# Weight splits and adaLN steps held in source order on VectorE, in a hybrid trunk block

## The chip, the cores and the metric

The kernel runs on one core of a Trainium2 chip. The time is device microseconds of one execution. Lower is better. One execution was also recorded by the hardware profiler; the rows shown below come from that record.

## The reference

One layer of a decoder trunk for 256 tokens of width 2048, all in f32. A conditioning vector c gives six modulation vectors (adaLN); the token mixer runs a retention branch and a short convolution branch side by side, and a gated feed-forward part with a causal convolution follows.

```python
mod = silu(c) @ w_ada + b_ada                      # 2048 x 12288
sh1, sc1, g1, sh2, sc2, g2 = split(mod, 6)
xn = rmsnorm(h, norm1_g) * (1 + sc1) + sh1
q, k, v, g_ret, bg, cg, xc, gates = split(xn @ w_in)
y_ret  = (retention(rotary(q), rotary(k), v) * silu(g_ret)) @ w_ret_o
y_conv = (bg * causal_conv3(cg * xc, w_sc)) @ w_conv_o
ga, gb = split(sigmoid(gates + b_gate))
h = h + g1 * ((ga * y_ret + gb * y_conv) @ w_mix_o)
xn2 = rmsnorm(h, norm2_g) * (1 + sc2) + sh2
gt = causal_conv3(xn2 @ w_gate, w_ffconv, b_ffconv)   # 5632 wide
h = h + g2 * ((silu(gt) * (xn2 @ w_up)) @ w_down)
out = rmsnorm(h, final_g)
```

## The kernel before

**Split products.** Every matrix product is made of rounded f32 pieces. A weight tile of 256 rows by 512 columns arrives in a buffer `raw` (SyncE's DMA queue, lines 291 and 323; six buffers). ScalarE rounds it into `hi` (L300), VectorE takes the rest, `lo = raw - hi` (L301). TensorE multiplies with both. Activations are split in the same way by `split` (L92 on ScalarE, L93 on VectorE).

**Units.** The program is a list of units, walked by one loop. A `Weights` unit is one such tile with its products. In `w_block` a unit issues, for each of four outputs, two matmuls with `hi` (L405, 512 columns) and two with `lo` (L410, 256 columns). Eight units make a block of 512 output columns; after the last unit ScalarE copies half of each output out of PSUM (L416) and an `epilogue` runs for each of the four. An `Ada` unit multiplies a weight tile of w_ada by the conditioning vector and adds it to an accumulator `ada` on VectorE (L335 for the first row tile, L337 for the others); it has no products on TensorE. Ada units are spread between the others until the second norm. A `Call` unit runs a helper.

**Stages.** Ten blocks in the first stage (values, swish gate, first query and key block), then the other query and key blocks with retention, the merge gates with the retention output, the convolution branch, the merge gates with the convolution output (`conv_o_block`, L797 to L800, then a split L92 and L93), the mixer output, the second norm, and the feed-forward part: eleven pairs of a gate block and an up block (`ff_blocks`, epilogues `e_g` L912 to L921 and `e_u` L924 to L926) and two rounds of down blocks.

**What sets the order.** The loop loads nine units ahead and calls `prep` (the casts and differences) two units ahead of `run`, in the first stage four ahead. So in the source the `lo` of unit n+2 is written after the products and the epilogue of unit n-1 and before those of unit n. The framework then reorders the instructions of each engine by when it reckons their operands to be ready. Each engine takes its instructions in the order that results. `tc.keep_in_program_order(x)` holds x behind the instruction that was written just before it for the same engine; it adds no wait for data.

The pools `hi` and `lo` have three buffers each, so `hi` and `lo` can be at most three units ahead of the products.

Of the kernel before, what the change touches and what calls it, by code (L numbers as in the profile page):

```python
# [10 lines left out]
F32 = mybir.dt.float32  # L11
# [4 lines left out]
ALU = mybir.AluOpType  # L16
# [30 lines left out]
def tile_trunk_block(  # L47
# [6 lines left out]
    nc = tc.nc  # L54
# [16 lines left out]
    def nm(s):  # L71
        serial[0] += 1
        return f"{s}_{serial[0]}"
# [7 lines left out]
    def blk8(name, shape, dtype):  # L81
        return big.tile(shape, dtype, tag="b8", name=nm(name))
# [43 lines left out]
    c_act = const.tile([P, KT], F32, name="c_act")  # L126
# [140 lines left out]
    class Call:  # L267
# [6 lines left out]
        def prep(self):  # L274
            if self.fn["prep"]:
                self.fn["prep"]()
# [5 lines left out]
    class Weights:  # L282
# [10 lines left out]
        def prep(self):  # L293
            if self.in_big:
                both = blk8("hl", [P, 2, UK, CB], F32R)
                self.hi, self.lo = both[:, 0], both[:, 1]
            else:
                self.hi = wpool.tile([P, UK, CB], F32R, tag="hi", bufs=3, name=nm("hi"))
                self.lo = wpool.tile([P, UK, CB], F32R, tag="lo", bufs=3, name=nm("lo"))
            nc.scalar.copy(self.hi, self.raw)  # L300
            nc.vector.tensor_tensor(self.lo, self.raw, self.hi.bitcast(F32), op=ALU.subtract)  # L301

        def run(self):
            self.run_(self)
# [1 line left out]
    class Ada:  # L306
# [23 lines left out]
        def prep(self):  # L330
            acc = self.state["acc"]
            for k in range(self.nk):
                kt = self.k0 + k
                if kt == 0 and not self.bias:
                    nc.vector.tensor_scalar_mul(acc, self.raw[:, k], c_act[:, 0:1])  # L335
                    continue
                nc.vector.scalar_tensor_tensor(  # L337
                    acc, self.raw[:, k], c_act[:, kt:kt + 1], acc, op0=ALU.mult, op1=ALU.add
                )
            if self.k0 + self.nk == KT:  # L340
                self.done(acc)

# [727 lines left out]
```

## Time and profile before

| | |
|---|---|
| time, median of 3 runs | 1924.78 us (1922.29 to 1925.09) |
| the profiled execution | 1922.16 us, its span in the trace 1920.3 us |
| TensorE busy | 1872.8 us, 98% of the span |
| VectorE busy | 1366.4 us, 71% |
| ScalarE busy | 904.9 us, 47% |
| data moved | 450.88 MB, mean 235 GB/s |

The span is the part of the execution that the trace covers; 1.9 us lie around it. In the rows further down a time in square brackets is how long the engine stood idle before the instruction, with what ended it.

### The profile page before, as it was taken

How to read it: one execution, taken by the hardware profiler on the slowest of the kernel's cores; microseconds unless marked ns; L12 is line 12 of the kernel's file. 1: busy time of each engine (PE TensorE's matmuls, PEld its weight loads, DVE VectorE, ACT ScalarE, POOL GpSimd, SP SyncE). 2: the span in 40 equal slices, each digit the busy share in tenths (PEclk: the TensorE clock that was granted, in tenths of full speed). 3: DMA queues.
4: the chain of work that ended last, by engine and by line, in shares of the span. 5: the costliest groups of instructions: out<-in, count | busy, mean ns of one | idle time of the engine just before them, and what ended most of it. 6: DMA issues, size and time to landing. Idle time of an engine off the chain costs nothing.

```text
span 1920.3 us, 26558 instructions
## 1 busy us (share of the span) xinstructions
PE 1872.8 (98%) x10151; PEld 1609.6 (84%) x10151; DVE 1366.4 (71%) x1690; ACT 904.9 (47%) x1187; POOL 22.4 (1%) x52
## 2 busy tenths in 40 slices
PE   4999999999999999999999999999999999999998
PEld 3788888888888888888888787888888888888886
DVE  6889987776676777778777786666665456666655
ACT  3544444444444444444445445555554335555543
POOL 1000000000000000000000000000000000000000
PEclk9899999999999999999999999999999999999999
DMA  8989865666878788787888994666665666666653
GB/s 302 322 305 333 290 218 191 192 199 210 271 267 270 260 271 262 255 283 261 272 274 290 315 318 154 186 187 185 194 192 189 195 190 194 187 189 192 209 195 124
DMA packets 220288, 450.88 MB, mean 235 GB/s; under 512 B 14516, under 2 KB 23040, under 8 KB 219648
## 3 DMA queue, kind: packets, MB, share of 16 engines
q1 hardware_dynamic: 218784, 445.84, 70.8%
q10 hardware_dynamic: 864, 3.15, 0.4%
q8 instruction: 79, 1.29, 0.3%
q14 instruction: 49, 0.40, 0.1%
q0 software_dynamic: 512, 0.20, 0.0%
HBM read 447.03 MB, written 2.10 MB: 234 GB/s over the span
## 4 chain that ended last, share of the span: by engine, by line
PE 90%; DVE 4%; DMA 3%; issue 2%; ACT 1%; POOL 0%; SPq 0%; POOLq 0%; DVEq 0%; ACTq 0%
PE acc L405 42%; PE acc L410 21%; PE acc L373 8%; PE acc L374 8%; PE acc L372 8%; DMA raw<-in_w_ada 2%; DVE lo L301 1%; DVE ada L337 1%; PE misc L351 1%; PE acc L519 1%; PE acc L517 1%; PE acc L518 1%; DVE hl L301 0%; PE misc L247 0%; PE misc L653 0%
## 5 line engine op out<-in xcount | busy, mean ns | idle before, releaser
L300 ACT CAST hi<-raw 128x1024 fp32r<-128x1024 f32 x616 | 647.9, 1052 | 831.9 <-PE acc L405 537.6
L301 DVE TENSOR_TENSOR lo<-raw,hi 128x1024 fp32r<-128x1024 f32 x616 | 748.4, 1221 | 354.3 <-ACT hi L300 351.1
L405 PE MATMUL acc<-xn,hi 128*128 128x512 f32 x3072 | 968.6, 397 | 2.9 <-DVE xn L894 1.8
L410 PEld LDWEIGHTS acc<-xn,lo 128*128 128x128 f32 x3072 | 577.8, 188 | 136.6 <-DVE lo L301 0.2
L410 PE MATMUL acc<-xn,lo 128*128 128x256 f32 x3072 | 605.0, 278 | 0.0
L405 PEld LDWEIGHTS acc<-xn,hi 128*128 128x128 f32 x3072 | 468.8, 189 | 5.2 <-DVE xn L894 2.2
L337 DVE SCALAR_TENSOR_TENSOR ada<-raw,c_act,ada 128x1024 f32<-128x1024 f32 (+1 forms) x199 | 238.8, 1200 | 128.0 <-DMA raw<-in_w_ada 127.0
L372 PE MATMUL acc<-hi,ff_t 128*128 128x512 f32 x332 | 129.2, 389 | 0.0
L373 PE MATMUL acc<-lo,ff_t 128*128 128x512 f32 x332 | 129.2, 389 | 0.0
L374 PE MATMUL acc<-hi,ff_t 128*128 128x512 f32 x332 | 129.1, 389 | 0.0
L416 ACT COPY sb<-acc 128x256 f32<-128x256 f32 x224 | 82.5, 368 | 44.9 <-PE acc L410 37.7
L405 PE MATMUL acc<-y_t,hi 128*128 128x512 f32 x256 | 80.5, 396 | 0.0
L405 PE MATMUL acc<-conv_t,hi 128*128 128x512 f32 x256 | 80.4, 395 | 0.0
L374 PEld LDWEIGHTS acc<-hi,ff_t 128*128 128x128 f32 x332 | 62.3, 188 | 13.0
L372 PEld LDWEIGHTS acc<-hi,ff_t 128*128 128x128 f32 x332 | 62.3, 188 | 13.0
L373 PEld LDWEIGHTS acc<-lo,ff_t 128*128 128x128 f32 x332 | 62.3, 188 | 12.7
L373 PE MATMUL acc<-lo,xn 128*128 128x512 f32 x172 | 69.0, 401 | 1.6 <-DVE lo L301 1.5
L372 PE MATMUL acc<-hi,xn 128*128 128x512 f32 x172 | 68.0, 403 | 2.0 <-ACT hi L300 2.0
L374 PE MATMUL acc<-hi,xn 128*128 128x512 f32 x172 | 68.4, 398 | 0.0
L410 PEld LDWEIGHTS acc<-y_t,lo 128*128 128x128 f32 x256 | 47.9, 188 | 13.7 <-DVE lo L301 2.5
L410 PEld LDWEIGHTS acc<-conv_t,lo 128*128 128x128 f32 x256 | 48.0, 188 | 12.9 <-DVE lo L301 1.6
L410 PE MATMUL acc<-y_t,lo 128*128 128x256 f32 x256 | 50.5, 279 | 1.8 <-DVE lo L301 1.8
(204 smaller groups left out, 1619.4 us busy)
## 6 DMA issues: line engine op xcount, KB each, us to landing
raw<-in_w_in SPq DMA_DIRECT2D x288, 512.0 KB, 4.8
raw<-in_w_ada SPq DMA_DIRECT2D x176, 512.0 KB, 4.8
raw<-in_w_gate SPq DMA_DIRECT2D x88, 512.0 KB, 4.4
raw<-in_w_up SPq DMA_DIRECT2D x88, 512.0 KB, 4.4
raw<-in_w_down SPq DMA_DIRECT2D x88, 512.0 KB, 4.4
raw<-in_w_ret_o SPq DMA_DIRECT2D x32, 512.0 KB, 4.7
raw<-in_w_conv_o SPq DMA_DIRECT2D x32, 512.0 KB, 5.4
raw<-in_w_mix_o SPq DMA_DIRECT2D x32, 512.0 KB, 5.6
```

What stands on the lines that cost most here:

```text
L300: nc.scalar.copy(self.hi, self.raw)
L301: nc.vector.tensor_tensor(self.lo, self.raw, self.hi.bitcast(F32), op=ALU.subtract)
L337: nc.vector.scalar_tensor_tensor(acc, self.raw[:, k], c_act[:, kt:kt + 1], acc, op0=ALU.mult, op1=ALU.add)
L351: nc.tensor.matmul(ps[:, i:i + 1], lhsT=flat[:, (s0 + i) * P:(s0 + i + 1) * P], rhs=ones[:, 0:1], start=True, stop=True,)
L372: nc.tensor.matmul(ps, lhsT=xh, rhs=u.hi[:, k, :], start=k0 + k == first, stop=False)
L373: nc.tensor.matmul(ps, lhsT=xh, rhs=u.lo[:, k, :], start=False, stop=False)
L374: nc.tensor.matmul(ps, lhsT=xl, rhs=u.hi[:, k, :], start=False, stop=k0 + k == end - 1)
L405: nc.tensor.matmul(ps, lhsT=u.hi[:, k, i * P:(i + 1) * P], rhs=xt(k0 + k).rearrange("p h s -> p (h s)"), start=k0 + k == 0, stop=False,)
L410: nc.tensor.matmul(ps[:, 0:S], lhsT=u.lo[:, k, i * P:(i + 1) * P], rhs=xt(k0 + k)[:, 0, :], start=False, stop=last and k == UK - 1,)
L416: nc.scalar.copy(b, ps[:, S:2 * S])
L517: nc.tensor.matmul(ps, lhsT=wh, rhs=xk[:, 0, :], start=first, stop=False)
L518: nc.tensor.matmul(ps, lhsT=wh, rhs=xk[:, 1, :], start=False, stop=False)
```

## The change

Three instructions of VectorE are held in the order of the source: the `lo` difference (L301) and both forms of the adaLN step (L335, L337). No instruction is added or removed on any engine. 648 differences and 208 adaLN steps are concerned.

```diff
--- before.py
+++ after.py
@@ -298,7 +298,8 @@
                 self.hi = wpool.tile([P, UK, CB], F32R, tag="hi", bufs=3, name=nm("hi"))
                 self.lo = wpool.tile([P, UK, CB], F32R, tag="lo", bufs=3, name=nm("lo"))
             nc.scalar.copy(self.hi, self.raw)
-            nc.vector.tensor_tensor(self.lo, self.raw, self.hi.bitcast(F32), op=ALU.subtract)
+            tc.keep_in_program_order(
+                nc.vector.tensor_tensor(self.lo, self.raw, self.hi.bitcast(F32), op=ALU.subtract))
 
         def run(self):
             self.run_(self)
@@ -332,11 +333,12 @@
             for k in range(self.nk):
                 kt = self.k0 + k
                 if kt == 0 and not self.bias:
-                    nc.vector.tensor_scalar_mul(acc, self.raw[:, k], c_act[:, 0:1])
+                    tc.keep_in_program_order(
+                        nc.vector.tensor_scalar_mul(acc, self.raw[:, k], c_act[:, 0:1]))
                     continue
-                nc.vector.scalar_tensor_tensor(
+                tc.keep_in_program_order(nc.vector.scalar_tensor_tensor(
                     acc, self.raw[:, k], c_act[:, kt:kt + 1], acc, op0=ALU.mult, op1=ALU.add
-                )
+                ))
             if self.k0 + self.nk == KT:
                 self.done(acc)
```

The orders below are those of the built programs. In the program after, lines are numbered one or two higher (L302 is the old L301, L339 the old L337, L407 and L412 the old L405 and L410, L914 to L923 the old L912 to L921, L799 to L802 the old L797 to L800).

VectorE at the end of the second gate block of the feed-forward part, before. `lo_11286`, `lo_11312` and `lo_11334` belong to the third, fourth and fifth unit after that block's last one; `ffg` and `ffy` are the epilogue's tiles, `ffs` is ScalarE's sigmoid.

```order
L916 SCALAR_TENSOR_TENSOR ffy_11245<-ffg_11243,vec_t,ffy_11245 128x256 x2
L914 SCALAR_TENSOR_TENSOR ffy_11245<-ffg_11243,vec_t,ffy_11245 128x256
L912 TENSOR_TENSOR ffg_11243<-acc_11082,sb_11274 128x256
L916 SCALAR_TENSOR_TENSOR ffy_11245<-ffg_11243,vec_t,ffy_11245 128x256
L301 TENSOR_TENSOR lo_11286<-raw_11099,hi_11285 128x1024
L914 SCALAR_TENSOR_TENSOR ffy_11245<-ffg_11243,vec_t,ffy_11245 128x256
L301 TENSOR_TENSOR lo_11312<-raw_11121,hi_11311 128x1024
L916 SCALAR_TENSOR_TENSOR ffy_11245<-ffg_11243,vec_t,ffy_11245 128x256
L301 TENSOR_TENSOR lo_11334<-raw_11143,hi_11333 128x1024
L921 TENSOR_TENSOR ffy_11245<-ffy_11245,ffs_11280 128x1024
L301 TENSOR_TENSOR lo_11356<-raw_11165,hi_11355 128x1024
```

The same place after.

```order
L916 SCALAR_TENSOR_TENSOR ffy_11245<-ffg_11243,vec_t,ffy_11245 128x256 x2
L918 SCALAR_TENSOR_TENSOR ffy_11245<-ffg_11243,vec_t,ffy_11245 128x256 x2
L916 SCALAR_TENSOR_TENSOR ffy_11245<-ffg_11243,vec_t,ffy_11245 128x256
L914 TENSOR_TENSOR ffg_11243<-acc_11082,sb_11274 128x256
L918 SCALAR_TENSOR_TENSOR ffy_11245<-ffg_11243,vec_t,ffy_11245 128x256
L916 SCALAR_TENSOR_TENSOR ffy_11245<-ffg_11243,vec_t,ffy_11245 128x256
L918 SCALAR_TENSOR_TENSOR ffy_11245<-ffg_11243,vec_t,ffy_11245 128x256
L923 TENSOR_TENSOR ffy_11245<-ffy_11245,ffs_11280 128x1024
L302 TENSOR_TENSOR lo_11286<-raw_11099,hi_11285 128x1024
L302 TENSOR_TENSOR lo_11312<-raw_11121,hi_11311 128x1024
L302 TENSOR_TENSOR lo_11334<-raw_11143,hi_11333 128x1024
```

The first `lo` moved behind the whole epilogue, L923 with its wait for the sigmoid included.

TensorE at the third unit after the gate block, before.

```order
L410 MATMUL acc_11292<-xn_1925_10584,lo_11234 128x256 x2
L405 MATMUL acc_11289<-xn_1937_10627,hi_11285 128x512 x2
L410 MATMUL acc_11289<-xn_1937_10627,lo_11286 128x256 x2
L405 MATMUL acc_11290<-xn_1937_10627,hi_11285 128x512 x2
L410 MATMUL acc_11290<-xn_1937_10627,lo_11286 128x256 x2
L405 MATMUL acc_11291<-xn_1937_10627,hi_11285 128x512 x2
L410 MATMUL acc_11291<-xn_1937_10627,lo_11286 128x256 x2
L405 MATMUL acc_11292<-xn_1937_10627,hi_11285 128x512 x2
L410 MATMUL acc_11292<-xn_1937_10627,lo_11286 128x256 x2
L405 MATMUL acc_11289<-xn_1937_10627,hi_11311 128x512 x2
```

The same place after.

```order
L412 MATMUL acc_11292<-xn_1925_10584,lo_11234 128x256 x2
L407 MATMUL acc_11289<-xn_1937_10627,hi_11285 128x512 x2
L407 MATMUL acc_11290<-xn_1937_10627,hi_11285 128x512 x2
L407 MATMUL acc_11291<-xn_1937_10627,hi_11285 128x512 x2
L407 MATMUL acc_11292<-xn_1937_10627,hi_11285 128x512 x2
L412 MATMUL acc_11289<-xn_1937_10627,lo_11286 128x256 x2
L412 MATMUL acc_11290<-xn_1937_10627,lo_11286 128x256 x2
L412 MATMUL acc_11291<-xn_1937_10627,lo_11286 128x256 x2
L412 MATMUL acc_11292<-xn_1937_10627,lo_11286 128x256 x2
L407 MATMUL acc_11289<-xn_1937_10627,hi_11311 128x512 x2
```

The eight `hi` products of the unit now stand ahead of its eight `lo` products. This form stands at 27 places in the program after, all of them units whose `lo` follows an epilogue: at the eleven gate blocks of the feed-forward part and at 16 blocks of the mixer. In the program before it stands nowhere.

VectorE at the end of the third block of `conv_o_block`, before. `lo_9408` is the second unit after the block's last one.

```order
L301 TENSOR_TENSOR lo_9408<-raw_9269,hi_9407 128x1024
L797 TENSOR_TENSOR sb_9370<-acc_9196,sb_9370 128x256
L797 TENSOR_TENSOR sb_9379<-acc_9197,sb_9379 128x256
L799 TENSOR_TENSOR gate_9163<-gate_9163,sb_9370 128x256
L799 TENSOR_TENSOR gate_9163<-gate_9163,sb_9379 128x256
L800 TENSOR_TENSOR gate_9163<-gate_9163,mixp_5098 128x256 x2
L797 TENSOR_TENSOR sb_9388<-acc_9198,sb_9388 128x256
L797 TENSOR_TENSOR sb_9397<-acc_9199,sb_9397 128x256
L799 TENSOR_TENSOR gate_9163<-gate_9163,sb_9388 128x256
L799 TENSOR_TENSOR gate_9163<-gate_9163,sb_9397 128x256
L800 TENSOR_TENSOR gate_9163<-gate_9163,mixp_5098 128x256 x2
L301 TENSOR_TENSOR lo_9434<-raw_9288,hi_9433 128x1024
```

The same place after, from the last output's adds on.

```order
L799 TENSOR_TENSOR sb_9388<-acc_9198,sb_9388 128x256
L802 TENSOR_TENSOR gate_9163<-gate_9163,mixp_5098 128x256
L801 TENSOR_TENSOR gate_9163<-gate_9163,sb_9388 128x256
L799 TENSOR_TENSOR sb_9397<-acc_9199,sb_9397 128x256
L802 TENSOR_TENSOR gate_9163<-gate_9163,mixp_5098 128x256
L801 TENSOR_TENSOR gate_9163<-gate_9163,sb_9397 128x256
L802 TENSOR_TENSOR gate_9163<-gate_9163,mixp_5098 128x256
L93 TENSOR_TENSOR mixed_9402<-gate_9163,mixed_9402 128x4x256
L302 TENSOR_TENSOR lo_9408<-raw_9269,hi_9407 128x1024
L302 TENSOR_TENSOR lo_9434<-raw_9288,hi_9433 128x1024
```

Here too the `lo` moved behind the epilogue and behind its L93, which takes ScalarE's L92 cast.

## Rows read from the trace of the kernel before

**Rows 1.** The page, busy time by engine

```profile
PE 1872.8 (98%) x10151; PEld 1609.6 (84%) x10151; DVE 1366.4 (71%) x1690; ACT 904.9 (47%) x1187; POOL 22.4 (1%) x52
```

**Rows 2.** Busy time by stretch: stretch, length, engines, clock, DMA share, GB/s

```profile
1190.00:1500.00 310.00, 310.00 (x1714) 268.17 (x1713) 200.09 (x259) 158.66 (x202) 0.64 (x6) 1.00 0.61 190
1500.00:1890.00 390.00, 390.00 (x2019) 332.85 (x2018) 239.60 (x284) 189.29 (x228) 0.32 (x3) 1.00 0.62 195
```

**Rows 3.** Waits of TensorE, whole span: total us, times, longest

```profile
PE acc L373 <- DVE lo L301: 3.2, 4, 1.2
PE acc L410 <- DVE lo L301: 3.0, 2, 1.8
```

**Rows 4.** Waits of VectorE, whole span

```profile
DVE ada L337 <- DMA raw<-in_w_ada: 127.0, 84, 5.5
```

**Rows 5.** Timeline of VectorE at a gate block's end: start, length, instruction

```profile
1340.33 1.22 DVE L301 TENSOR_TENSOR lo<-raw,hi 128x1024 fp32r<-128x1024 f32 x1
1341.47 0.48 DVE L914 SCALAR_TENSOR_TENSOR ffy<-ffg,vec_t,ffy 128x256 f32<-128x256 f32 x1
...
1344.79 1.22 DVE L921 TENSOR_TENSOR ffy<-ffy,ffs 128x1024 f32<-128x1024 f32 x1
```

**Rows 6.** Timeline of ScalarE, same place

```profile
1338.63 2.20 ACT L300 CAST hi<-raw 128x1024 fp32r<-128x1024 f32 x2
1340.73 0.59 ACT L913 ACTIVATE ffy<-ffg,vec_t 128x256 f32<-128x256 f32 x1
...
1343.57 1.06 ACT L920 ACTIVATE ffs<-ffy 128x1024 f32<-128x1024 f32 x1
```

**Rows 7.** Timeline of TensorE, same place

```profile
1337.02 0.63 PE L405 MATMUL acc<-xn,hi 128*128 128x512 f32 x2
...
1342.59 0.63 PE L405 MATMUL acc<-xn,hi 128*128 128x512 f32 x2
1343.06 0.39 PE L410 MATMUL acc<-xn,lo 128*128 128x256 f32 x2
```

**Rows 8.** Timeline of VectorE at a conv_o block's end

```profile
1037.42 0.75 DVE L800 TENSOR_TENSOR gate<-gate,mixp 128x256 f32<-128x256 f32 x2
1038.09 2.35 DVE L301 TENSOR_TENSOR lo<-raw,hi 128x1024 fp32r<-128x1024 f32 x2
1040.36 1.21 DVE L93 TENSOR_TENSOR mixed<-gate,mixed 128x1024 fp32r<-128x1024 f32 x1
```

**Rows 9.** Timeline of ScalarE, same place

```profile
1036.28 1.05 ACT L300 CAST hi<-raw 128x1024 fp32r<-128x1024 f32 x1 [0.67 <-PE acc L405]
1038.20 1.05 ACT L92 CAST mixed<-gate 128x1024 fp32r<-128x1024 f32 x1 [0.87 <-DVE gate L800]
```

**Rows 10.** Timeline of TensorE, same place

```profile
1036.27 0.63 PE L405 MATMUL acc<-xn,hi 128*128 128x512 f32 x2
```

**Rows 11.** Timeline of VectorE, rotation of a query block

```profile
334.24 1.23 DVE L626 TENSOR_TENSOR rot<-qk,cos_t 128x1024 f32<-128x1024 f32 x1
...
337.83 0.69 DVE L628 TENSOR_TENSOR rotated<-rot,qk 128x512 f32<-128x512 f32 x1
```

**Rows 12.** Timeline of VectorE and TensorE, late adaLN data

```profile
1074.65 1.28 DVE L337 SCALAR_TENSOR_TENSOR ada<-raw,c_act,ada 128x1024 f32<-128x1024 f32 x1 [3.29 <-DMA raw<-in_w_ada]
...
1075.85 1.22 DVE L301 TENSOR_TENSOR lo<-raw,hi 128x1024 fp32r<-128x1024 f32 x1
...
1077.13 0.50 PE L410 MATMUL acc<-conv_t,lo 128*128 128x256 f32 x2 [1.19 <-DVE lo L301]
```

**Rows 13.** Short stretches with waits of TensorE, columns as in rows 2

```profile
476.00:478.00 2.00, 0.40 (x2) 0.00 (x0) 2.00 (x2) 0.78 (x1) 0.00 (x0) 1.00 0.01 5
```

**Rows 14.** Short stretches at the second norm, columns as in rows 2

```profile
1178.00:1180.00 2.00, 0.69 (x2) 0.60 (x3) 2.00 (x7) 1.31 (x3) 0.00 (x0) 0.87 0.00 0
1180.00:1182.00 2.00, 2.00 (x8) 1.71 (x8) 2.00 (x7) 1.31 (x3) 0.00 (x0) 0.50 0.00 0
1182.00:1184.00 2.00, 2.00 (x11) 1.67 (x11) 1.19 (x4) 0.28 (x1) 0.00 (x0) 0.77 0.00 0
```

## The prediction

> **What bounds the kernel now.** I read the busy times first: TensorE works 98% of the span, VectorE 71%, ScalarE 47% [rows 1]. A share is only an average, so I looked at stretches next: from 1190 us to 1890 us, the whole feed-forward part, TensorE is busy in every microsecond [rows 2]. There it is the bound, and whatever makes it wait is added to the end time one for one. The waits of TensorE come third: in the whole span it waits for the difference `lo` only 3.2 us (four times) at L373 and 3.0 us (twice) at L410 [rows 3]. So today `lo` is hardly ever late, and VectorE has 29% of idle time. The last view is the waits of VectorE: 127 us, in 84 pieces, go to data of w_ada that hasn't landed [rows 4]. Those waits cost nothing unless a `lo` is queued behind them that TensorE needs soon.
>
> So little can be won: at most those 6.2 us, and the question is what the later place of `lo` costs.
>
> **What the change moves.** It removes and adds no instruction. VectorE does the same work in another order, TensorE's order follows it at 27 places, and SyncE's queue holds the same loads. A `lo` now stands behind the whole epilogue that was written ahead of it. TensorE has a reserve for this: when a block ends, the next unit or two have their `lo` ready.
>
> **The gate blocks of the feed-forward part (eleven).** Take the one in [rows 5 to 7]. TensorE ends the block's last unit and starts the next at 1337.02, and the third unit after the block starts at 1342.59, two units of 2.785 us later; its first `lo` product is at 1343.06. Before, that `lo` was made at 1340.33, in the gaps between the epilogue's operations: the last output's L914 came only at 1341.47 since ScalarE did two casts (2.20 us from 1338.63) and then L913 (0.59 us from 1340.73), which ends at 1341.32. After, the `lo` must wait for the chain of that last output:
> - L914 starts at about 1341.35 and takes 0.48, L916 as long: 1342.35 with the hand-over;
> - L920, the sigmoid on ScalarE, 1.06 us: 1343.45. In the new order of ScalarE it stands ahead of the next cast, and ScalarE is free, so nothing else delays it;
> - L921, 1.22 us: 1344.75;
> - the `lo`, 1.22 us: 1345.95.
>
> TensorE isn't idle until then, since it now takes the eight `hi` products of the unit first. They last 8 x 0.232 = 1.85 us (in the old order two of them and two of `lo` follow each other in 0.70 us, of which the `hi` pair has 0.47), up to 1344.44. The wait is 1345.95 - 1344.44 = 1.5 us, 1.6 with a semaphore. Without the new order of TensorE it would be 3 us. Eleven blocks: **17.6 us**. From both sides: 0.8 us each if the epilogue runs ahead of the row times because no `lo` is mixed into it (8.8), 3 us each if the `hi` products don't cover (33). I take 1.6, which is made from this row's own durations.
>
> **The conv_o blocks (four).** Here the `lo` of the second unit after the block moves behind L93, and so behind ScalarE's L92, which stands behind a cast. TensorE starts that unit at 1036.27 [rows 10] and its eight `hi` products end at 1038.12. ScalarE's cast of another unit runs from 1036.28 for 1.05 us [rows 9], since it waits for its buffer, so L92 can begin at 1037.35 at the earliest and ends at 1038.4. L93 takes 1.21 [rows 8]: 1039.65. Then the `lo`, 1.2: 1040.85. The wait is 2.7 us, four times **10.8 us**; between 1.5 each (if L92 gets ahead of the cast, less 1.05 us and a hand-over) and 3.9 each (if the block that follows takes other shapes and the `hi` products cover nothing more): 6 to 15.6.
>
> **The rotations (two places).** Four operations follow the end of the block before `lo`, 1.23, 1.23, 0.69 and 0.69 us [rows 11] (L627 and L629 are as long as L626 and L628). With a copy and an add of 0.4 each, and `lo` of 1.22, that is 5.9 us, against a reserve of one unit and eight `hi` products, 2.785 + 1.85 = 4.64. The wait is 1.2 us, with hand-overs 1.5; two times **3 us**.
>
> **The other eleven places of the new order, and the rest.** They are convolution and retention epilogues, with reserves of one or two units. The trace doesn't show the wait; from the nearest rows it lies between 0 (the reserve covers, as it does by a margin where two units are ready) and 1.6 us (as in the gate blocks). Most of these epilogues lack the sigmoid, whose two operations make 2.3 us of that chain, so I take 0.7: **7.7 us**, between 0 and 17.6. The first `lo` of the second part of the input, near 62 us, moves behind two L93 and their casts: 0 to 5 us, I take **2.5**.
>
> **What the moved adaLN steps give.** They move back by four places on average. At 1074.65 VectorE had waited 3.29 us for adaLN data; the `lo` behind it came at 1075.85, and TensorE waited 1.19 us for it [rows 12]. All waits of TensorE for `lo` at L373 and L410 together are 6.2 us, of which 5.4 may go: **-5.4 us**, between 0 and -6.2. The adaLN data itself is late by DMA, and nobody else waits for the accumulators until the norm. A buffer of `raw` comes free later by the same 1 to 4 us; in the feed-forward part the DMA engines are busy 61 to 62% [rows 2], so I put that at nothing; were DMA full, each late load would bring its wait again.
>
> **The clock.** A wait of 1.79 us within 476 to 478 left the granted clock at 1.00 [rows 13]. At the second norm TensorE waited twice in a row, and the clock went to 0.50, that is 1.2 GHz, for 1180 to 1182 and 0.77 after [rows 14], which lost 0.26 + 1.00 + 0.46 = 1.7 us. Waits of 1.6 us that stand a gate and an up block apart (16 units of 2.785, some 45 us) are like the first of these rows, so the sum holds nothing for the clock. The Trainium skill ("TensorE: Matmul & The Clock Gate", section "HAM oscillation — how this bites in real kernels") says that a TensorE which waits between bursts of matmuls again and again can fall back to half clock each time, and starts each burst slow. [...]
>
> **Sum.** 17.6 + 10.8 + 3 + 7.7 + 2.5 - 5.4 = +36.2 us. The profiled execution took 1922.16 (span 1920.3 and 1.9 around it): 1958.4. The median of the three runs lies 2.6 above it, so I forecast **1961 us**.
>
> **Rivals.**
> 1. *The reserve covers more.* The epilogues run closer together without a `lo` mixed in, all waits are at their low ends: 8.8 + 6 + 0 + 0 + 0 - 5.4 = +9.4, 1934 us. For it: VectorE has 29% idle. Against: the chain of the gate block is made of waits for ScalarE, and these don't get shorter.
> 2. *The other side: late adaLN data no longer stands in front of `lo`.* Place: the blocks with adaLN units up to the second norm; price -6.2 us at most, so 1919 us. It decides only if all the new waits together stay below 6 us, so below 0.35 us at each gate block and nothing elsewhere: the `lo` of [rows 5] would have to come 1.2 us before the working above.
> 3. *The clock falls at each wait.* 27 places by 1.7 us add 46 us: 2007 us; if only the long waits at conv_o and half of the gate blocks trip it, 10 x 1.7 = 17: 1978. For it: [rows 14]; against: [rows 13]. [...]
> 4. *The order does nothing*, since the `lo` was on time by a wide margin: 1925 us. In [rows 7] the margin is 1.5 us (1341.55 to 1343.06), and the shift of `lo` is 4.4 us, so I hold it for unlikely.
>
> **How the numbers follow.** The forecast has 0.63, rival 1 0.18, rival 2 0.04, rival 3 0.12, rival 4 0.03. The range goes from rival 1 to somewhat above the middle form of rival 3: 1936 to 1985; it leaves out rivals 2 and 4, the lower half of rival 1 and the upper end of rival 3. About 0.2% (4 us) is what a measurement of this kernel can tell from no change. Faster by more: rival 2's 0.04; within: rival 4's 0.03 and a little of rival 1, 0.04; slower: 0.92.
>
> **What would show it.** In the new trace the eleven gate blocks each show a wait of TensorE for `lo` at the first `lo` product of the third unit, 1.6 us, right after an L921; the conv_o blocks one of 2.7 behind L93. VectorE's total stays 1366 us. TensorE's busy share falls to about 96%. If the waits are there but much shorter, the reserve was mis-sized; if the time is longer than their sum, look at the clock and at late `raw` data.

## The result and the profile after

The changed kernel takes 2002.58 us (median of 4 runs) against 1924.89 us before: a ratio of 1.0407, 95% interval 1.0389 to 1.0425, so 78 us more. The sign was forecast, the size was not: 36 us were forecast. The profiled execution of the changed kernel has a span of 2001.6 us.

The page after, busy time by engine, and the waits of TensorE (total, times, longest), to be read beside [rows 1] and [rows 3]:

```profile
PE 1900.0 (95%) x10151; PEld 1622.0 (81%) x10151; DVE 1380.2 (69%) x1690; ACT 902.7 (45%) x1187; POOL 21.4 (1%) x52
```

```profile
PE acc L412 <- DVE lo L302: 36.1, 25, 2.6
...
PE acc L375 <- DVE lo L302: 12.0, 5, 4.2
PE misc L353 <- DVE ada L339: 7.0, 3, 4.9
PE acc L374 <- ACT hl L300: 5.4, 3, 3.3
PE acc L374 <- ACT hi L300: 5.1, 2, 2.8
PE acc L519 <- ACT hl L300: 3.6, 1, 3.6
PE acc L519 <- ACT hi L300: 2.8, 1, 2.8
```

TensorE's idle time grew from 47.5 us (1920.3 - 1872.8) to 101.6 (2001.6 - 1900.0): 54 us. Its busy time grew by 27 us though it has the same 10151 instructions; some 19 of these are a lower granted clock, added up further down. Waits for `lo` went from 6.2 us to 48.1. The last four rows are waits for ScalarE's casts: 16.9 us, and 7.0 us in the trace before. Two of these casts, at 49 and 56 us, had waited for their data (4.7 us of TensorE's time); four others (12.0 us) stand behind the norm's own work in ScalarE's order.

The input is normed in five parts, here called chunks; a chunk change is the place in the first stage where the next part is normed between the units. Both traces do the same matmuls in nearly the same order, so I compared the times at which each trace starts its n-th matmul. The difference grows like this (good to some 1 us):

| up to, in the trace before | what it is | difference so far, us |
|---|---|---|
| 30 us | the head, up to the first chunk | 4 |
| 74 | the first chunk change | 8.5 |
| 142 | the chunk change near 126 to 130 | 18 |
| 217 | the chunk change near 180 to 190 | 21.5 |
| 251 | rotary table, last chunk change | 30 |
| 317 | end of the first stage | 30.5 |
| 707 | query, key, retention, its output | 36 |
| 905 | convolution | 42 |
| 1111 | conv_o and the start of the mixer output | 57 |
| 1195 | up to the feed-forward part | 57 |
| 1746 | feed-forward up to the tenth gate block | 77 |
| 1800 | the eleventh gate block | 78.5 |
| 1898 | the last down blocks | 81 |

**The first stage cost 29 us, where 2.5 were forecast.** VectorE at the chunk change after:

```profile
133.05 1.28 DVE L339 SCALAR_TENSOR_TENSOR ada<-raw,c_act,ada 128x1024 f32<-128x1024 f32 x1
...
136.42 0.17 DVE L360 TENSOR_TENSOR b<-misc,vec_t 128x4 f32<-128x4 f32 x1 [1.49 <-PE misc L353]
...
139.01 0.69 DVE L93 TENSOR_TENSOR xn<-x_t,xn 128x512 fp32r<-128x512 f32 x1 [1.10 <-ACT xn L92]
140.97 0.69 DVE L93 TENSOR_TENSOR xn<-x_t,xn 128x512 fp32r<-128x512 f32 x1 [1.27 <-ACT xn L92]
141.58 1.22 DVE L302 TENSOR_TENSOR lo<-raw,hi 128x1024 fp32r<-128x1024 f32 x1
```

The last adaLN step is followed by a chain VectorE, TensorE (L353), VectorE, ScalarE, VectorE (two L93). The next `lo` is held behind all of it, 7 us after that step ended, and VectorE stands idle for most of that time. In the trace before two differences ran ahead of the first L93 (at 128.70) of the same chunk, and TensorE worked on them while the norm ran:

```profile
125.25 1.22 DVE L301 TENSOR_TENSOR lo<-raw,hi 128x1024 fp32r<-128x1024 f32 x1
...
127.20 1.21 DVE L301 TENSOR_TENSOR lo<-raw,hi 128x1024 fp32r<-128x1024 f32 x1
```

After, it runs out of them. It waits first for a cast that stands behind the norm's activations (L443) on ScalarE, then for the held `lo`:

```profile
136.89 1.58 ACT L443 ACTIVATE x_t<-x_t,b,a 128x256 f32<-128x256 f32 x3 [3.92 <-DVE a L365]
...
139.39 1.03 ACT L300 CAST hi<-raw 128x1024 fp32r<-128x1024 f32 x1
```

```profile
140.47 0.58 PE L519 MATMUL acc<-xn,hi 128*128 128x256 f32 x1 [2.81 <-ACT hi L300]
...
142.85 0.58 PE L521 MATMUL acc<-xn,lo 128*128 128x256 f32 x1 [1.17 <-DVE lo L302]
```

A `raw` buffer comes free only with its `lo`, so SyncE's queue has nothing to load into. Its issues, and busy time by stretch at the same place (columns as in [rows 2]):

```profile
134.36 0.37 SPq L324 DMA_DIRECT2D raw<-in_w_ada  x1
142.86 0.37 SPq L291 DMA_DIRECT2D raw<-in_w_in  x1
```

```profile
130.00:136.00 6.00, 6.00 (x34) 4.92 (x33) 4.93 (x6) 1.40 (x2) 0.00 (x0) 1.00 0.97 330
136.00:142.00 6.00, 2.88 (x15) 2.25 (x14) 2.81 (x7) 5.11 (x9) 0.00 (x0) 0.68 0.36 138
142.00:148.00 6.00, 5.15 (x24) 5.15 (x25) 6.00 (x6) 2.03 (x3) 0.00 (x0) 0.50 0.64 209
```

For 8.5 us no load is issued and the loads fall from 330 GB/s to 138; TensorE idles 3 of 6 us, and then runs at a granted clock of 0.50, the lower of its two levels. That the missing loads cost time isn't shown: from 75 us to the end of the stage no wait of TensorE above 0.25 us in this trace is for a cast that had waited for data, and from 148 to 200 us it is busy all the time. Once the head is behind, the trace before has no wait of TensorE for ScalarE in this stage.

**The gate blocks did what was forecast.** VectorE and TensorE at one of them, with the chain of [rows 5] and [rows 6]:

```profile
1314.12 0.48 DVE L916 SCALAR_TENSOR_TENSOR ffy<-ffg,vec_t,ffy 128x256 f32<-128x256 f32 x1 [0.95 <-ACT ffy L915]
1314.64 0.48 DVE L918 SCALAR_TENSOR_TENSOR ffy<-ffg,vec_t,ffy 128x256 f32<-128x256 f32 x1
1316.31 1.23 DVE L923 TENSOR_TENSOR ffy<-ffy,ffs 128x1024 f32<-128x1024 f32 x1 [1.19 <-ACT ffs L922]
1317.45 3.49 DVE L302 TENSOR_TENSOR lo<-raw,hi 128x1024 fp32r<-128x1024 f32 x3
```

```profile
1315.35 2.00 PE L407 MATMUL acc<-xn,hi 128*128 128x512 f32 x8
1318.72 1.21 PE L412 MATMUL acc<-xn,lo 128*128 128x256 f32 x8 [1.37 <-DVE lo L302]
```

Eight `hi` products, then a wait for the `lo` that had to stand behind L923. Ten of the eleven gate blocks have such a wait, 1.37 to 1.40 us, the first 2.62.

**The conv_o blocks cost more than their wait.** TensorE, and the granted clock in the stretch behind it:

```profile
1035.15 2.00 PE L407 MATMUL acc<-xn,hi 128*128 128x512 f32 x8
1039.61 2.08 PE L412 MATMUL acc<-xn,lo 128*128 128x256 f32 x8 [2.45 <-DVE lo L302]
```

```profile
1037.00:1039.00 2.00, 0.15 (x1) 0.00 (x0) 1.81 (x2) 0.16 (x1) 0.00 (x0) 1.00 0.00 0
1039.00:1041.00 2.00, 1.39 (x6) 1.40 (x7) 2.00 (x3) 1.05 (x1) 0.00 (x0) 0.56 0.20 28
1041.00:1043.00 2.00, 2.00 (x10) 1.76 (x9) 2.00 (x3) 0.00 (x0) 0.00 (x0) 0.59 0.91 313
```

The eight `lo` products take 2.08 us here and 1.21 at the gate block: after this wait the clock is about half. The first conv_o block has a wait of the same length, and its clock stays at 1.00:

```profile
992.13 1.22 PE L412 MATMUL acc<-xn,lo 128*128 128x256 f32 x8 [2.45 <-DVE lo L302]
```

```profile
993.00:995.00 2.00, 2.00 (x13) 1.78 (x13) 2.00 (x3) 0.29 (x1) 0.00 (x0) 1.00 0.83 246
```

### The profile page after: what moved, and what is told of

It reads as the page before. It is cut to its first block, busy times and chain, and to the rows that moved or that the text cites. A ratio compares the mean times of both kernels' runs of the same rounds, so it can differ in the third digit from the quotient of the medians.

```text
span 2001.6 us, 26574 instructions
## 1 busy us (share of the span) xinstructions
PE 1900.0 (95%) x10151; PEld 1622.0 (81%) x10151; DVE 1380.2 (69%) x1690; ACT 902.7 (45%) x1187; POOL 21.4 (1%) x52
## 5 line engine op out<-in xcount | busy, mean ns | idle before, releaser
L302 DVE TENSOR_TENSOR lo<-raw,hi 128x1024 fp32r<-128x1024 f32 x616 | 742.0, 1223 | 400.4 <-ACT hi L300 399.8
L407 PE MATMUL acc<-xn,hi 128*128 128x512 f32 x3072 | 956.9, 397 | 1.8 <-DVE xn L896 1.8
L412 PEld LDWEIGHTS acc<-xn,lo 128*128 128x128 f32 x3072 | 566.1, 190 | 174.2 <-DVE lo L302 50.1
L412 PE MATMUL acc<-xn,lo 128*128 128x256 f32 x3072 | 598.1, 281 | 36.1 <-DVE lo L302 36.1
L407 PEld LDWEIGHTS acc<-xn,hi 128*128 128x128 f32 x3072 | 477.9, 190 | 11.7 <-DVE xn L896 2.6
L339 DVE SCALAR_TENSOR_TENSOR ada<-raw,c_act,ada 128x1024 f32<-128x1024 f32 (+1 forms) x199 | 238.8, 1200 | 4.6 <-DMA raw<-in_w_ada 3.4
L407 PE MATMUL acc<-y_t,hi 128*128 128x512 f32 x256 | 80.5, 396 | 0.0
L407 PE MATMUL acc<-conv_t,hi 128*128 128x512 f32 x256 | 80.4, 395 | 0.0
L412 PEld LDWEIGHTS acc<-conv_t,lo 128*128 128x128 f32 x256 | 47.8, 188 | 12.0 <-DVE lo L302 1.3
L412 PEld LDWEIGHTS acc<-y_t,lo 128*128 128x128 f32 x256 | 48.2, 188 | 11.3
L375 PE MATMUL acc<-lo,mixed 128*128 128x512 f32 x128 | 51.4, 401 | 4.1 <-DVE lo L302 4.1
```

Of the source, the lines that this page charges most:

```text
L339: tc.keep_in_program_order(nc.vector.scalar_tensor_tensor(acc, self.raw[:, k], c_act[:, kt:kt + 1], acc, op0=ALU.mult, op1=ALU.add))
L375: nc.tensor.matmul(ps, lhsT=xh, rhs=u.lo[:, k, :], start=False, stop=False)
L407: nc.tensor.matmul(ps, lhsT=u.hi[:, k, i * P:(i + 1) * P], rhs=xt(k0 + k).rearrange("p h s -> p (h s)"), start=k0 + k == 0, stop=False,)
L412: nc.tensor.matmul(ps[:, 0:S], lhsT=u.lo[:, k, i * P:(i + 1) * P], rhs=xt(k0 + k)[:, 0, :], start=False, stop=last and k == UK - 1,)
```

## The experiments

The theory after the result (A): each place has its own chain, the `lo` held behind it costs TensorE a wait there, and in the first stage it also holds back `raw` buffers and so the loads. Rivals: the held adaLN steps cost the first stage; the stages share a loss; the sigmoid or the split is not in the chain. In the edits, `held(c)` is `tc.keep_in_program_order` where c is true and leaves the instruction free otherwise. Ratios stand against the kernel before on the same chip; they come from all runs of both and can differ from the quotient of the two medians by up to 0.1%, which is 1.9 us. What comes back is a difference of two ratios and has some 5 us to either side.

### The first stage alone

```diff
-            tc.keep_in_program_order(
+            held(at_prep[0] < n_start)(
                 nc.vector.tensor_tensor(self.lo, self.raw, self.hi.bitcast(F32), op=ALU.subtract))
```

The same at both forms of the adaLN step.

> Differences and adaLN steps are held in source order only while the first stage is prepared; the later stages have the order of before. Theory A (in the first stage the differences of a new chunk stand behind the norm's two L93, which wait through TensorE and ScalarE, so the raw buffers are given back late and the next weights land late; in later stages the differences stand behind epilogues): the first stage alone loses what the two traces differ by at its end, +29 us, so 1954 us. Theory B (the loss in the first stage comes from a clock or a load level that the later stages share, and the stages can't be told apart): the loss is not 29 but near 78 or near 0.

Measured: 1949.50 us against 1920.40, ratio 1.0154 (1.0133 to 1.0175), +29 us. By the count of matmuls 28 us are there at 251 us, nothing is added after, and some 2 are given back. The first stage's loss is its own.

### The later stages alone

```diff
-            tc.keep_in_program_order(
+            held(at_prep[0] >= n_start)(
                 nc.vector.tensor_tensor(self.lo, self.raw, self.hi.bitcast(F32), op=ALU.subtract))
```

The same at the adaLN steps.

> Differences and adaLN steps are held from the end of the first stage on only. Theory A (the loss is a sum over stages, and the first stage alone costs 29 us as measured): the rest, 47 to 50 us over before, ratio 1.0245 to 1.026. Theory B (the stages share something, such as raw buffers that stay late): the two parts do not add up, off by 8 us or more.

Measured: 1971.28 us against 1921.14, ratio 1.0252 (1.0238 to 1.0266), +48.4 us. With the 29 of the first stage that is 77.5, the whole of the change's 78. The stages add up.

### The adaLN steps alone

```diff
-            tc.keep_in_program_order(
+            held(False)(
                 nc.vector.tensor_tensor(self.lo, self.raw, self.hi.bitcast(F32), op=ALU.subtract))
```

> Only the adaLN steps are held; no difference is. In the built order the differences at the chunk changes of the first stage stand as before, while from the second stage on the differences stand behind the epilogues all the same, at the same 27 places as in the change. Theory A: the first stage loses nothing (0 to 3 us), the rest loses 49 to 54 us, so 1974 to 1979 us. Theory B (the held adaLN steps, by holding their raw buffers longer, are what costs the first stage): about the whole loss, 1995 to 2003 us.

Measured: 1921.36 us against 1920.40, ratio 1.0004 (0.9994 to 1.0014). Both expectations are wrong: the order of later stages that they name is not the one that ran. In the trace of this run the differences of the gate blocks stand between the epilogue's operations as in [rows 5]:

```profile
1342.48 1.22 DVE L306 TENSOR_TENSOR lo<-raw,hi 128x1024 fp32r<-128x1024 f32 x1
1343.61 0.48 DVE L920 SCALAR_TENSOR_TENSOR ffy<-ffg,vec_t,ffy 128x256 f32<-128x256 f32 x1
1344.01 1.23 DVE L306 TENSOR_TENSOR lo<-raw,hi 128x1024 fp32r<-128x1024 f32 x1
```

So the held differences cost the 78 us, and the rival that blames the adaLN steps falls, all but for 6 us (the differences held alone were not run). By the count of matmuls this run is 6 us late at 111 us and gives some 4 back between 400 and 1195 us. Where the 6 come from, VectorE and TensorE at the head of this run:

```profile
26.63 0.26 DVE L122 COPY vec_t<-misc 128x96 f32<-128x96 f32 x1 [2.41 <-PE misc L121]
26.80 4.68 DVE L343 SCALAR_TENSOR_TENSOR ada<-raw,c_act,ada 128x512 f32<-128x512 f32 x6
```

```profile
31.54 1.86 PE L357 MATMUL misc<-ones,ada 128*128 128x1 f32 x8 [4.95 <-DVE ada L343]
```

Six adaLN steps stand behind a copy that waits for TensorE's turned vectors, and TensorE then waits 4.95 us for their sum. In the trace before they had run ahead of that copy:

```profile
19.17 7.83 DVE L337 SCALAR_TENSOR_TENSOR ada<-raw,c_act,ada 128x512 f32<-128x512 f32 x10
27.60 0.26 DVE L122 COPY vec_t<-misc 128x96 f32<-128x96 f32 x1 [0.60 <-PE misc L121]
```

### The adaLN steps alone, from the end of the first stage on

```diff
-                tc.keep_in_program_order(nc.vector.scalar_tensor_tensor(
+                held(at_prep[0] >= n_start)(nc.vector.scalar_tensor_tensor(
                     acc, self.raw[:, k], c_act[:, kt:kt + 1], acc, op0=ALU.mult, op1=ALU.add
```

The differences are free everywhere, as in the run above.

> Only the adaLN steps are held, and these only from the end of the first stage on; all differences are free. In the run with adaLN steps held everywhere the head lost 6 us and the stages up to the second norm gave 4 to 5 back. Theory A (the head's loss comes from the first adaLN steps behind a copy that waits for TensorE; later, adaLN steps that stand further back no longer hold up a difference while their data is late): 3 to 5 us faster than before, ratio 0.9974 to 0.9985. Theory B (what came back later was only the head's loss, since TensorE caught up with data that had come in the meantime): no gain, ratio 0.999 to 1.001.

Measured: 1916.01 us against 1921.14, ratio 0.9968 (0.9956 to 0.9980): 6 us faster than the kernel before, a little more than expected. This version beats both. By the count of matmuls it is 2 us ahead at 480, 3 at 905 and 6 at 1111, after the places where adaLN data was late, as in [rows 12]; another 1.5 come at the second norm, where the clock stayed up in this trace and fell in the one before. Its waits of TensorE for `lo`, at L379 alone, where before there were 3.2 and 3.0 us [rows 3]:

```profile
PE acc L379 <- DVE lo L306: 2.6, 4, 1.4
```

### The chunk changes of the first stage freed

```diff
+        def prep(self):
+            free[0] -= 1
...
-            tc.keep_in_program_order(
+            held(free[0] <= 0)(
                 nc.vector.tensor_tensor(self.lo, self.raw, self.hi.bitcast(F32), op=ALU.subtract))
...
                 split(xk, xn1[k // 4][:, k % 4:k % 4 + 2])
+            free[0] = 5
```

> As the change, but the differences of the first units behind each part of the norm in the first stage are not held; in the built order they stand between the norm's operations again. Theory A: 22 to 29 us of the first stage come back, 1974 to 1981 us. Theory B (it is the adaLN steps, or all differences of the first stage being a little later): under 8 us come back, 1995 to 2003 us.

Measured: 1988.31 us against 1920.40, ratio 1.0354 (1.0333 to 1.0376). Of the change's 4.07% that takes back 0.53%, 10 us: less than half of what theory A claimed, and with its 5 us to either side not clear of theory B's 8. The count of matmuls decides it: at 217 us this run is 8 us late where the change is 21.7. So the chunk changes are real, but not the whole. The rest shows in this trace: 6 of the 8 us are there by 111 us (the head, above), and it loses another 9 between 217 and 251 us, most of them at one wait. VectorE and TensorE there:

```profile
239.66 1.23 DVE L308 TENSOR_TENSOR hl<-raw,hl 128x1024 fp32r<-128x1024 f32 x1
240.81 0.42 DVE L145 TENSOR_TENSOR cos_t<-cos_t,rotary_room 128x256 f32<-128x256 f32 x1
241.14 2.35 DVE L308 TENSOR_TENSOR lo<-raw,hi 128x1024 fp32r<-128x1024 f32 x2
```

```profile
242.41 0.79 PE L381 MATMUL acc<-lo,xn 128*128 128x512 f32 x1 [6.64 <-DVE lo L308]
```

### The rotary table freed

In the changed kernel the second part of the rotary table stands in one piece ahead of the next `lo`; the table's steps (L145), TensorE, and the stretches there (columns as in [rows 2]):

```profile
244.85 0.29 DVE L145 TENSOR_SCALAR rotary_room<-cos_t 128x256 f32<-128x256 f32 x1
...
252.14 0.43 DVE L145 TENSOR_TENSOR cos_t<-cos_t,rotary_room 128x256 f32<-128x256 f32 x1
252.48 2.35 DVE L302 TENSOR_TENSOR lo<-raw,hi 128x1024 fp32r<-128x1024 f32 x2
```

```profile
253.76 0.50 PE L375 MATMUL acc<-lo,xn 128*128 128x512 f32 x1 [4.21 <-DVE lo L302]
```

```profile
250.00:255.00 5.00, 1.24 (x4) 1.01 (x5) 4.79 (x10) 0.00 (x0) 0.00 (x0) 0.92 0.04 8
255.00:260.00 5.00, 4.59 (x16) 3.48 (x15) 2.24 (x6) 2.14 (x3) 0.00 (x0) 0.50 0.88 297
```

Here VectorE is busy all the time, loads stop (8 GB/s), TensorE waits, and its clock is 0.50 for the next 5 us.

```diff
     def rest_of_rotary():
...
+        free[0] = 5
```

with the `lo` held where `free[0] <= 0`, as above.

> As the change, but the differences of the first units behind the second part of the rotary table are not held, so that they stand between the table's steps again. Theory A (some 20 steps of the table stand in one piece ahead of the differences, TensorE waits 4.2 us for one, the raw buffers come free late and the clock falls after it): 8 to 12 us of the change's loss go, ratio to before 1.035 to 1.037. Theory B (the loss at this place is made by the norm of the last part, which stands beside it): under 3 us, ratio 1.039 to 1.041.

Measured: 1991.44 us against 1921.14, ratio 1.0359 (1.0343 to 1.0374): 9 us come back, as theory A had it. By the count of matmuls this run loses 2 us between 217 and 251 us, where the change loses 8.

### The gate block's sigmoid three units later

```diff
             if i == 3:
-                sg = w4("ffs", [P, 4, S])
-                nc.scalar.activation(sg, st["y"], AF.Sigmoid)
-                nc.vector.tensor_tensor(st["y"], st["y"], sg, op=ALU.mult)
+                after(3, swish_g)   # the same three lines
```

> As the change, but the sigmoid and the product that close a gate block of the feed-forward part are written three units later, so that the difference no longer stands behind them. Theory A (at the gate blocks TensorE waits 1.6 us for a difference that stands behind the sigmoid and the product): 15 to 18 us of the change's loss go, 1985 to 1988 us. Rival C (the wait there is made of ScalarE's casts, and the sigmoid is not in the chain): no gain, 2000 to 2004 us.

Measured: 1986.99 us against 1920.40, ratio 1.0347 (1.0330 to 1.0365): 0.60% or 11.5 us come back; less than expected, far from no gain. By the count of matmuls the stretch 1195 to 1800 us loses 2.5 us in this run against 21.5 in the changed kernel, so 19 come back at the eleven gate blocks themselves; this run was 2 us later than the changed kernel ahead of them and lost 1.6 more at the last down blocks. VectorE at a gate block, where the `lo` is now ahead of the product:

```profile
1312.88 0.48 DVE L918 SCALAR_TENSOR_TENSOR ffy<-ffg,vec_t,ffy 128x256 f32<-128x256 f32 x1
1313.28 3.49 DVE L302 TENSOR_TENSOR lo<-raw,hi 128x1024 fp32r<-128x1024 f32 x3
1316.68 1.22 DVE L926 TENSOR_TENSOR ffy<-ffy,ffs 128x1024 f32<-128x1024 f32 x1
```

### The split of conv_o three units later

```diff
                 mixed.append(mb)
-                split(store["g"], mb)
+                if j < 3:
+                    after(3, lambda: split(store["g"], mb))
+                else:
+                    split(store["g"], mb)
```

> As the change, but the split (L92, L93) that closes the first three conv_o blocks is written three units later, so that the differences no longer stand behind it. Theory A (TensorE waits 2.45 us at each for a difference behind L93, and runs at half clock for a while after it): 8 to 9.5 us of the loss go, ratio 1.035 to 1.037. Rival (the adds of the epilogue make the wait, and the split is hidden): under 3 us, ratio 1.039 to 1.041.

Measured: 1990.77 us against 1921.14, ratio 1.0358 (1.0342 to 1.0374): 9.4 us for three places, 3.1 each, of which 2.45 is the wait. By the count of matmuls the change loses 2.9, 4.2 and 4.4 us at the three: the first is the one whose clock stayed up. TensorE has no wait left between 950 and 1100 us.

### All four edits

> As the change, with the edits of e3, e4, e5 and e6 together. Theory A (the places cost each their own wait, so their losses add up): the four gains sum to 40 to 45 us of the change's 78, which leaves 33 to 38 us, ratio 1.017 to 1.020. Theory B (a wait that is taken away at one place is made up for at the next): under 30 us come back, ratio 1.025 or more.

Measured: 1952.24 us against 1923.70, ratio 1.0149 (1.0132 to 1.0166): 2.58%, 49.6 us come back, more than the 40 to 45 that theory A gave (40 by the four ratios, 55 by the four counts of matmuls). Each of the ratios in that sum is uncertain by some 0.17%, 3.3 us, which covers the difference. Theory B falls. Of the 29 us left, 6 are the head's adaLN steps; the others lie, by the count, at the rotations (5), the convolution (8), and the last down blocks (4).

## Why the prediction was wrong

**Right: what bounds the kernel, and the mechanism.** TensorE is the bound, nothing hides a wait in it, and a `lo` behind an epilogue makes it wait. Chance 0.92 was put on slower. VectorE's total is 1380.2 us where 1366 was to stay; why isn't known.

**Right: the gate blocks.** 17.6 us were forecast, 1.6 each. Ten waits of 1.37 to 1.40 and one of 2.62 make 16.5; the repeat of the gate blocks, 46.23 us from one such wait to the next, is 1.67 longer than 16 units of 2.785. In the lines above the first `lo` product comes 3.37 us after the first `hi` product; the working has 3.36. By the count of matmuls the eleven cost 21.5 us, of which the first takes 4.1; why that one waits longer isn't known.

**Wrong: the first stage. This is the step that failed.** The term "the first `lo` of the second part of the input ... 0 to 5 us, I take 2.5" stood for the whole stage, and the stage cost 29 us: 27 of the 42 us by which the forecast fell short. The place that it names was sized well (some 2 us between 62 and 74 us). The other places of the same kind had no term: the later chunk changes, the rotary table, and the adaLN steps behind a copy at the head. By the runs the norm of all chunks is 10 us (14 by the count of matmuls), the rotary table 9 (6.5 by the count), the head 6 to 7 (the two runs with adaLN steps held alone differ by 0.36%). Some 11 of the 29 us are the lower clock (TensorE's busy time, times the missing share of the clock, is 20.8 us in this stage against 9.3 before), the others idle time.

The sentence "a buffer of `raw` comes free later ..., so I put that at nothing" looked at DMA in the feed-forward part, at 61% share. In the first stage the late `lo` does stop the loads, for 8.5 us at the chunk change shown. That this adds to the loss isn't shown: TensorE's waits there are for casts and differences behind the norm and the table; its waits for casts that had waited for data are 4.7 us, all before 60 us, against 2.0 before the change.

**Right in the wait, short in the price: conv_o.** 2.7 each were forecast, 2.45 and for the last 4.07 measured; by the count of matmuls the four cost 15 us, where 10.8 were forecast. The working let L92 begin at 1037.35 though [rows 8] has the last L800 end at 1038.17. It came out since the adds run closer together when no `lo` is mixed in, which the working didn't say.

**Wrong: "the sum holds nothing for the clock".** It held for ten gate blocks; at two of the three conv_o waits of 2.45 us, at the first gate block and ahead of the mixer output the clock went to 0.50. Summed over the trace from the second stage on, TensorE's busy time times the missing share of the clock is 9.5 us against 1.7 before. The Trainium skill ("TensorE: Matmul & The Clock Gate", section "HAM oscillation — how this bites in real kernels") describes a TensorE that falls to half clock while it waits between bursts and starts the next one slow; the waits of its example are longer than those forecast here. The trace agrees for the wait of 4.07 us. It agrees for two of the three waits of 2.45 us (0.56 and 0.59 behind the one shown) and for none of 1.4 us. So rival 3 was true for some places, at 1.7 us each and 3.4 after the longest wait.

**Rotations and the other places.** 3 + 7.7 us were forecast for them; the later stages alone, up to the end of the convolution, lost 13, with the gain of the adaLN steps already taken off. The last down blocks, which no term held, lost 2.7 more: TensorE waits 2.37 us there for a `lo`.

**The gain.** -5.4 us were forecast for the adaLN steps that move back. Held alone, from the second stage on, they give 6 us, and the waits of TensorE for `lo` behind late adaLN data (1.79, 1.19 and 1.18 us) are gone. This term was right, and it is the only part of the change that pays.

**Sum.** Forecast by stage: 2.5 in the first, 33.7 in the others. Measured: 29 and 48.4. The range ended at 1985 us, 18 short; the first stage alone was 26 more than its term. In rival 2 the limit for each gate block is 6 us over eleven, 0.55 us, and not 0.35.

## What to carry to other kernels

When an instruction is held in source order, look at every instruction written ahead of it on that engine, and price those that wait for another engine and those that are long (the rotary table's steps are 7.6 us): the held one stands behind all of it. List the places stage by stage: here the chain was priced rightly where it was looked for, and most of what was missing came from places of the same kind that no term held. A late instruction also gives its buffer back late, which stopped the loads for 8.5 us; whether that costs time must be read from what the bounding engine then waits for. What is only fed by late data and needed by nobody soon (here the adaLN steps) is the better thing to hold back, behind the work that others wait for.

## What the runs showed of the hardware

Behind a wait of TensorE the granted clock either stayed at 1.00 or fell to 0.50 for a while, and from the second stage on one such fall cost 1.7 us. The waits of 1.4 us at the gate blocks brought none in five traces with ten of them each. The 4.07 us ahead of the mixer output brought one or two in all seven traces that have it. Between these the same wait went either way from trace to trace: 2.01 us at a rotation, four traces of seven; 2.45 us at the first, second and third conv_o block, none, two and five of five; 2.62 to 2.65 us at the first gate block, four of five; 2.37 us at the last down blocks, two of seven. At the second norm two shorter waits stand close together (0.25 to 0.74 and 1.75 us), and the clock fell in four of eleven traces. So the length of the wait alone doesn't decide. What does was not tried by itself.
